# A decoder trunk on one core: the weight tiles and four sums move by 1728 bytes in SBUF, to the offset of h

## The chip, the cores and the metric

The kernel runs on one core of a Trainium2 chip. The metric is the device time of one execution in microseconds (us). Before the change it is 2354.61 us, the median of three runs (2351.29, 2354.61, 2356.11).

## The reference

Two layers of a decoder over 256 tokens of width 2048, all in float32. Layer 0 mixes tokens with a causal Conformer convolution, layer 1 with gated linear attention (GLA); each mixer is followed by a SwiGLU feed-forward net (FFN) of width 5632. Norms stand before and after each, and a vector `c` gives shifts, scales and gates.

```python
def swiglu_ffn(h, w_in, w_out):
    gate, up = jnp.split(h @ w_in, 2, axis=-1)
    return (jax.nn.silu(gate) * up) @ w_out

def reference(x, c, w_ada, b_ada, ...):
    c_act = jax.nn.silu(c)
    for i in range(DEPTH):
        mod = c_act @ w_ada[i] + b_ada[i]
        sh1, sc1, gt1, sh2, sc2, gt2 = jnp.split(mod[:, None, :], N_MOD, axis=-1)
        h = rms_norm(x, pre_mix_g[i]) * (1.0 + sc1) + sh1
...
            y = conformer_conv(h, ...)   # i even
...
            y = gla_mixer(h, ...)        # i odd
        x = x + gt1 * rms_norm(y, post_mix_g[i])
        h = rms_norm(x, pre_ffn_g[i]) * (1.0 + sc2) + sh2
        y = swiglu_ffn(h, ffn_w_in[i], ffn_w_out[i])
        x = x + gt2 * rms_norm(y, post_ffn_g[i])
    return x
```

## The kernel before

**Layout.** Activations lie transposed: 128 features to the partitions, 16 blocks `k` of features, 256 tokens along a row. The modulated input of each product, `h`, is kept as two float32r parts, a high one and the low rest, side by side: `h[:, k, 0, :]` and `h[:, k, 1, :]`, 2048 bytes a block and partition, 32768 in all. The FFN's inner result `m` and the GLA's gated output `oo` have the same form.

**Weights.** All weights come in tiles of 1 MB, `raw`, 128 partitions of 8192 bytes, in an order made up front by `tile_order`. Six buffers of the pool `rawp` hold them; every seventh tile of the first 130 goes to a buffer of its own in another pool (`cv`), far behind. `cast_upto` cuts a tile into two halves of eight 128x128 blocks, and splits each half: ScalarE writes the high part `hi` (L398), VectorE the rest `lo` (L399). The pools `hip` and `lop` have three buffers of 4096 bytes each. Tiles of `w_ada` take another way: VectorE multiplies them by `cb` and sums the rows (L364).

**Products.** `product` (L423 to L486) multiplies block by block. For a block of weights it issues two matmuls (L484): `hi` as the stationary operand against high and low part of the activations, 512 columns wide, and `lo` against the high part alone, 256 wide. This document calls them a wide and a narrow matmul, and both together a pair. The order of the two turns with each `k`, so that the two wide matmuls of neighbouring blocks stand next to each other, and the two narrow ones. The blocks of a half are 512 bytes apart in `hi` and `lo`; in the stage `r` the block of `k` is number `k` modulo 8 of its half. The first eight output blocks of four products (`pw2`, `in00`, `aqk`, `in10`) are packed: three matmuls of 256 columns each for a block (L439 to L441), 384 in a stage. In the first product, `pw1`, and in `v` the roles change: `h` is the stationary operand and `hi` or `lo` moves, 512 columns wide (L855 to L862, L1088 to L1090).

**Stages.** `pw1`, convolution, `pw2`; FFN of layer 0 (`in00`, `out00`, `in01`, `out01`); GLA (`aqk`, gates, `v` with the scores `s`, `r` with the attention `po`, `wo`); FFN of layer 1. Between them stand junctions, which renew `x` and make the next `h`. A matmul of float32 operands, such as `po`, stands twice in the trace, one record for each of its two passes.

**Where tiles lie.** The pool `const` is laid out in the order of its tiles, and the pools `rawp`, `hip`, `lop` and `tmp` follow. Bytes from a partition's start, in the program before: `h` 61024; then `masks` (1024 bytes), `inv_d`, `two_d`, `inv_e`, `mhalf` (32 each, with what they are rounded up by), `der` (512) and `ab` (64), 1728 together; then the sums `s_y`, `s_z`, `s_xz`, `s_xx` (1024 each) from 95520; the six `raw` buffers from 99616, three `hi` from 148768, three `lo` from 161056. The separate `raw` buffer is at 212640, `m` at 183904, `oo` at 190048, `cb` at 52064. Modulo 2048, `h`, `m` and `oo` start at 1632, and `raw`, `hi` and `lo` at 1312.

Of the kernel before, what the change touches and what calls it, by code (L numbers as in the profile page):

```python
# [7 lines left out]
F32 = mybir.dt.float32  # L8
F32R = mybir.dt.float32r
I8 = mybir.dt.int8  # L10
# [4 lines left out]
P = 128  # L15
D = 2048
KD = D // P
# [130 lines left out]
def trunk(ctx: ExitStack, tc: tile.TileContext, a: dict, out: bass.AP):  # L148
    nc = tc.nc

    const = ctx.enter_context(tc.tile_pool(name="const", bufs=1))
    rawp = ctx.enter_context(tc.tile_pool(name="rawp", bufs=6))
    hip = ctx.enter_context(tc.tile_pool(name="hip", bufs=3))
    lop = ctx.enter_context(tc.tile_pool(name="lop", bufs=3))
    tmp = ctx.enter_context(tc.tile_pool(name="tmp", bufs=2))
    ps = ctx.enter_context(tc.tile_pool(name="ps", bufs=4, space=PSUM))
    ps2 = ctx.enter_context(tc.tile_pool(name="ps2", bufs=1, space=PSUM))
# [27 lines left out]
    mod = const.tile([P, 2 * 6 * KD], F32, tag="mod", name="mod")  # L185
    h = const.tile([P, KD, 2, T], F32R, tag="h", name="h")
    h_hi, h_lo = h[:, :, 0, :], h[:, :, 1, :]
    masks = const.tile([P, 8, P], I8, tag="masks", name="masks")
    for j in range(4):
        s = slice(j * 512, (j + 1) * 512)  # L190
        pc = ps.tile([P, 512], F32, tag="mm", name=f"cb{j}")
# [10 lines left out]
    def cols(name, i, n):  # L202
        return par[:, COLS[name][0] + i : COLS[name][0] + i + n]

    inv_d = const.tile([P, 1], F32, tag="inv_d", name="inv_d")
    nc.vector.memset(inv_d, 1.0 / D)
    two_d = const.tile([P, 1], F32, tag="two_d", name="two_d")
    nc.vector.memset(two_d, 2.0 / D)
    inv_e = const.tile([P, 1], F32, tag="inv_e", name="inv_e")
    nc.vector.memset(inv_e, HEADS / D)  # L210
    mhalf = const.tile([P, 2], F32, tag="mhalf", name="mhalf")
    nc.vector.memset(mhalf, -0.5)
    der = const.tile([P, 8, KD], F32, tag="der", name="der")
    ab = const.tile([P, KD], F32, tag="ab", name="ab")

    s_y = const.tile([P, T], F32, tag="s_y", name="s_y")
    s_z = const.tile([P, T], F32, tag="s_z", name="s_z")
# [1034 lines left out]
```

## Time and profile before

| | before |
|---|---|
| runs, us | 2351.29, 2354.61, 2356.11 |
| profiled execution, us | 2356.34 |
| its span, us | 2354.6 |
| mean granted TensorE clock | 0.993 |
| DMA moved | 605.50 MB, mean 257 GB/s |

The span reaches from the first to the last instruction on the core; the profiled execution's own time is 1.7 us longer. PE is TensorE's matmul side and PEld its weight loads; DVE is VectorE, ACT ScalarE, POOL GpSimd. The duration of a matmul in the profile includes its way through the array, so neighbours overlap: what a matmul costs in a stream is the distance from its start to the next one's start, or a stretch of time divided by the matmuls that stand in it. In the rows of the timeline neighbours of one kind are put together: "x2" are two instructions, the first time is the start of the first.

### The profile page before, as it was taken

The numbers are of one execution on the slowest core, as the hardware profiler recorded it, in microseconds if no ns is written. First come the engines' busy times: TensorE is split into PE (matmuls) and PEld (weight loads), VectorE is DVE, ScalarE is ACT, GpSimd is POOL, SyncE is SP. The second block draws the span as 40 slices with busy tenths as digits, with TensorE's granted clock in tenths as the row PEclk, the third lists the DMA queues.
The fourth block names the chain that finished last, engine by engine and source line by source line (L and its number), as shares of the span: only waits on it lengthen the run. The fifth ranks groups of instructions, "written<-read, shape, count | busy, mean of one in ns | idle before, by whom it ended". The sixth has DMA issues, their size and how long they took to land.

```text
span 2354.6 us, 34894 instructions
## 1 busy us (share of the span) xinstructions
PE 2310.3 (98%) x14028; PEld 1999.0 (85%) x14028; DVE 1770.8 (75%) x2520; ACT 1113.3 (47%) x1677; POOL 26.4 (1%) x27
## 2 busy tenths in 40 slices
PE   8999999999999999999999999999999999999997
PEld 5777679998888888888898888889888888888886
DVE  5777859888877788889988878898666555666665
ACT  5333236654444444444456545554544444444442
POOL 0000000000000000000000000000000000000001
PEclk9999999999999999999999999999999999999998
DMA  9988967378878787888844556774565665665651
GB/s 379 418 334 336 377 270 291 139 268 310 312 295 320 300 316 295 318 302 308 300 162 161 215 217 228 259 260 148 212 228 204 230 228 204 230 228 203 231 192 59
DMA packets 85100, 605.50 MB, mean 257 GB/s; under 512 B 9573, under 2 KB 9957, under 8 KB 12101
## 3 DMA queue, kind: packets, MB, share of 16 engines
q1 hardware_dynamic: 84938, 603.28, 68.8%
q8 instruction: 110, 1.80, 0.3%
q14 instruction: 52, 0.43, 0.0%
HBM read 601.14 MB, written 2.10 MB: 256 GB/s over the span
## 4 chain that ended last, share of the span: by engine, by line
PE 94%; DVE 3%; ACT 1%; DMA 1%; issue 1%; POOL 0%; POOLq 0%; SPq 0%; DVEq 0%; ACTq 0%
PE in L484 38%; PE out L484 20%; PE r L484 4%; PE wo L484 4%; PE pw L484 2%; PE aqk L484 1%; PE v L1088 1%; PE v L1089 1%; PE v L1090 1%; PE s L1037 1%; PE in_pair L440 1%; PE in_pair L441 1%; PE in_pair L439 1%; DVE lo L399 1%; PE pw L861 1%; PE pw L862 1%
## 5 line engine op out<-in xcount | busy, mean ns | idle before, releaser
L398 ACT CAST hi<-raw 128x1024 fp32r<-128x1024 f32 x754 | 790.3, 1051 | 995.7 <-PE in L484 279.6
L399 DVE TENSOR_TENSOR lo<-raw,hi 128x1024 fp32r<-128x1024 f32 x754 | 919.6, 1222 | 453.6 <-ACT hi L398 452.6
L484 PE MATMUL in<-h,hi 128*128 128x512 f32 x2560 | 795.1, 392 | 0.2 <-DVE gate L938 0.2
L484 PEld LDWEIGHTS in<-h,lo 128*128 128x128 f32 x2560 | 480.7, 188 | 105.7
L484 PE MATMUL in<-h,lo 128*128 128x256 f32 x2560 | 505.2, 279 | 0.0
L484 PE MATMUL out<-m,hi 128*128 128x512 f32 (+1 forms) x1452 | 438.8, 385 | 0.0
L484 PEld LDWEIGHTS in<-h,hi 128*128 128x128 f32 x2560 | 388.0, 188 | 0.4 <-DVE gate L938 0.4
L364 DVE SCALAR_TENSOR_TENSOR raw<-raw,cb 128x2048 f32<-128x2048 f32 x159 | 362.8, 2284 | 0.0
L484 PEld LDWEIGHTS out<-m,lo 128*128 128x128 f32 x1408 | 263.5, 188 | 55.3 <-DVE lo L399 0.9
L484 PE MATMUL out<-m,lo 128*128 128x256 f32 x1408 | 281.0, 279 | 0.1
L484 PEld LDWEIGHTS out<-m,hi 128*128 128x128 f32 x1452 | 224.0, 188 | 2.1
L484 PE MATMUL wo<-oo,hi 128*128 128x512 f32 (+1 forms) x272 | 80.5, 379 | 1.4 <-ACT hi L398 1.4
L484 PE MATMUL r<-h,hi 128*128 128x512 f32 x256 | 81.6, 396 | 0.0
L498 DVE TENSOR_TENSOR join<-in,join 128x256 f32<-128x256 f32 x160 | 66.6, 416 | 0.0
L440 PE MATMUL in_pair<-h,hi 128*128 128x256 f32 x240 | 64.3, 279 | 0.7 <-DVE h L555 0.7
L441 PE MATMUL in_pair<-h,lo 128*128 128x256 f32 x240 | 62.6, 278 | 0.0
L439 PE MATMUL in_pair<-h,hi 128*128 128x256 f32 x240 | 59.3, 278 | 1.9 <-ACT h L554 1.9
L497 ACT COPY join<-in 128x256 f32<-128x256 f32 x160 | 58.4, 365 | 0.0
L484 PEld LDWEIGHTS wo<-oo,lo 128*128 128x128 f32 x256 | 47.9, 188 | 9.6
L484 PEld LDWEIGHTS r<-h,lo 128*128 128x128 f32 x256 | 47.7, 188 | 9.9
L484 PE MATMUL wo<-oo,lo 128*128 128x256 f32 x256 | 51.9, 279 | 0.0
L484 PE MATMUL r<-h,lo 128*128 128x256 f32 x256 | 51.7, 282 | 0.0
(424 smaller groups left out, 2841.9 us busy)
## 6 DMA issues: line engine op xcount, KB each, us to landing
raw<-in_in_dram SPq DMA_DIRECT2D x176, 1024.0 KB, 5.0
raw<-in_w_ada_dram SPq DMA_DIRECT2D x159, 1024.0 KB, 5.5
raw<-in_out_dram SPq DMA_DIRECT2D x88, 1024.0 KB, 5.1
raw<-in_pw_dram SPq DMA_DIRECT2D x48, 1024.0 KB, 8.3
raw<-in_aqk_dram SPq DMA_DIRECT2D x17, 1024.0 KB, 4.8
raw<-in_w_ada_s_dram SPq DMA_DIRECT2D x16, 1024.0 KB, 11.7
raw<-in_w_ada_r_dram SPq DMA_DIRECT2D x16, 1024.0 KB, 7.9
raw<-in_v_dram SPq DMA_DIRECT2D x16, 1024.0 KB, 4.8
```

Of the source, the lines that this page charges most:

```text
L364: nc.vector.scalar_tensor_tensor(out=raw, in0=raw, scalar=1.0, in1=cb, op0=ALU.mult, op1=ALU.mult, accum_out=modcol(name, i))
L398: nc.scalar.copy(hi, part)
L399: done = nc.vector.tensor_tensor(out=lo, in0=part, in1=hi.bitcast(F32), op=ALU.subtract)
L439: nc.tensor.matmul(acc, w_hi, x_hi, start=False, stop=False, skip_group_check=True)
L440: nc.tensor.matmul(acc, w_hi, x_lo, start=False, stop=False, skip_group_check=True)
L441: nc.tensor.matmul(acc, w_lo, x_hi, start=False, stop=closes, skip_group_check=True)
L484: nc.tensor.matmul(dst, weight, moving, start=n == 0 and i == 0, stop=end and i == len(parts) - 1, skip_group_check=ob not in narrow,)
L497: nc.scalar.copy(dst, acc[:, T:])
L498: nc.vector.tensor_tensor(out=dst, in0=acc[:, :T], in1=dst, op=ALU.add)
L861: nc.tensor.matmul(acc, h_hi[:, k, n], w_lo[:, s], start=False, stop=False, skip_group_check=shared)
L862: nc.tensor.matmul(acc, h_lo[:, k, n], w_hi[:, s], start=False, stop=k == KD - 1, skip_group_check=shared)
L1037: nc.tensor.matmul(sps[:, c], lhs[:, j, c], rhs[:, j, c], start=j == 0, stop=j == 1)
```

## The change

A new pool, `small`, stands behind `lop` and ahead of `tmp`. `masks`, `inv_d`, `two_d`, `inv_e`, `mhalf`, `der` and `ab` are taken from it in place of `const`.

```diff
     lop = ctx.enter_context(tc.tile_pool(name="lop", bufs=3))
+    small = ctx.enter_context(tc.tile_pool(name="small", bufs=1))
     tmp = ctx.enter_context(tc.tile_pool(name="tmp", bufs=2))
...
-    masks = const.tile([P, 8, P], I8, tag="masks", name="masks")
+    masks = small.tile([P, 8, P], I8, tag="masks", name="masks")
...
-    inv_d = const.tile([P, 1], F32, tag="inv_d", name="inv_d")
+    inv_d = small.tile([P, 1], F32, tag="inv_d", name="inv_d")
...
-    two_d = const.tile([P, 1], F32, tag="two_d", name="two_d")
+    two_d = small.tile([P, 1], F32, tag="two_d", name="two_d")
...
-    inv_e = const.tile([P, 1], F32, tag="inv_e", name="inv_e")
+    inv_e = small.tile([P, 1], F32, tag="inv_e", name="inv_e")
...
-    mhalf = const.tile([P, 2], F32, tag="mhalf", name="mhalf")
+    mhalf = small.tile([P, 2], F32, tag="mhalf", name="mhalf")
...
-    der = const.tile([P, 8, KD], F32, tag="der", name="der")
-    ab = const.tile([P, KD], F32, tag="ab", name="ab")
+    der = small.tile([P, 8, KD], F32, tag="der", name="der")
+    ab = small.tile([P, KD], F32, tag="ab", name="ab")
```

Every instruction stays: on each engine the same instructions stand in the same order with the same waits, and each has the same shapes. What differs is addresses. In bytes from a partition's start:

| tile | before | after | before, modulo 2048 | after, modulo 2048 |
|---|---|---|---|---|
| h | 61024 | 61024 | 1632 | 1632 |
| s_y | 95520 | 93792 | 1312 | 1632 |
| raw, first of six | 99616 | 97888 | 1312 | 1632 |
| hi, first of three | 148768 | 147040 | 1312 | 1632 |
| lo, first of three | 161056 | 159328 | 1312 | 1632 |
| masks | 93792 | 171616 | 1632 | 1632 |
| der | 94944 | 172768 | 736 | 736 |
| temporaries (`tmp`) | 173344 | 173344 | 1312 | 1312 |
| m | 183904 | 183904 | 1632 | 1632 |
| oo | 190048 | 190048 | 1632 | 1632 |
| separate raw | 212640 | 212640 | 1696 | 1696 |

1728 is 27 times 64 and three times 512 and 192 more. So the offset modulo 64 is the same for every tile (32 for those that move), and modulo 512 the weight blocks go from 192 bytes past those of `h` to the same offset.

## The prediction

> **What bounds the kernel.** The page first: the busy shares, and the chain of waits that ended last by engine.
>
> ```profile
> span 2354.6 us, 34894 instructions
> PE 2310.3 (98%) x14028; PEld 1999.0 (85%) x14028; DVE 1770.8 (75%) x2520; ACT 1113.3 (47%) x1677; POOL 26.4 (1%) x27
> PE 94%; DVE 3%; ACT 1%; DMA 1%; issue 1%; POOL 0%; POOLq 0%; SPq 0%; DVEq 0%; ACTq 0%
> ```
>
> TensorE matmuls are 98% of the span and 94% of the chain. So the time is the number of matmuls times the pace at which they follow each other. The number is not touched. The question is whether addresses set the pace, and the next view answers part of it: stretches of time with the matmuls that stand in each (the x behind PE's busy time; then PEld, DVE, ACT, POOL, clock, DMA share, GB/s).
>
> ```profile
> 50.00:340.00 290.00, 276.35 (x1703) 202.76 (x1702) 210.05 (x308) 95.63 (x139) 0.69 (x1) 0.98 0.88 351
> 808.00:1050.00 242.00, 242.00 (x1405) 212.93 (x1404) 195.66 (x229) 117.68 (x175) 0.00 (x0) 1.00 0.82 308
> 1973.00:2215.00 242.00, 242.00 (x1405) 213.08 (x1404) 153.31 (x189) 117.34 (x175) 0.00 (x0) 1.00 0.62 220
> ```
>
> The second and third row are the same stage of the two FFNs (`in01`, `in11`). PE never rests, and both have 1405 matmuls in 242 us: 172.2 ns a matmul, 344.5 ns a pair of wide and narrow. VectorE is busy 195.66 us in one and 153.31 in the other, the DMA engines 0.82 and 0.62 of the time. So other engines' traffic in SBUF doesn't reach TensorE's pace; if addresses do, it is by what TensorE reads itself: the moving operand, and the weights that it loads meanwhile.
>
> How many pairs this is about, by the groups of L484 (wide matmuls; some rows hold a few narrow ones):
>
> ```profile
> L484 PE MATMUL in<-h,hi 128*128 128x512 f32 x2560 | 795.1, 392 | 0.2 <-DVE gate L938 0.2
> L484 PE MATMUL out<-m,hi 128*128 128x512 f32 (+1 forms) x1452 | 438.8, 385 | 0.0
> L484 PE MATMUL wo<-oo,hi 128*128 128x512 f32 (+1 forms) x272 | 80.5, 379 | 1.4 <-ACT hi L398 1.4
> L484 PE MATMUL r<-h,hi 128*128 128x512 f32 x256 | 81.6, 396 | 0.0
> ```
>
> Together 4540. One ns a pair is 4.5 us, 0.2% of the time, which is about what a measurement of this kernel can tell from no change.
>
> **Is the pace a matter of offsets?** Here is TensorE's timeline in `r`. Each row is two neighbours; the pace is the distance between starts.
>
> ```profile
> 1432.15 0.39 PE L484 MATMUL r<-h,lo 128*128 128x256 f32 x2
> 1432.37 0.62 PE L484 MATMUL r<-h,hi 128*128 128x512 f32 x2
> 1432.83 0.40 PE L484 MATMUL r<-h,lo 128*128 128x256 f32 x2
> 1433.07 0.62 PE L484 MATMUL r<-h,hi 128*128 128x512 f32 x2
> 1433.53 0.28 PE L484 MATMUL r<-h,lo 128*128 128x256 f32 x1
> 1433.64 0.50 PE L507 MATMUL sso<-inv_e,s_z 128*128 128x1 f32 x4
> ...
> 1434.67 0.39 PE L484 MATMUL r<-h,lo 128*128 128x256 f32 x2
> 1434.89 0.62 PE L484 MATMUL r<-h,hi 128*128 128x512 f32 x2
> 1435.35 0.40 PE L484 MATMUL r<-h,lo 128*128 128x256 f32 x2
> 1435.59 0.62 PE L484 MATMUL r<-h,hi 128*128 128x512 f32 x2
> 1436.05 0.39 PE L484 MATMUL r<-h,lo 128*128 128x256 f32 x2
> ...
> 1436.73 0.40 PE L484 MATMUL r<-h,lo 128*128 128x256 f32 x2
> ```
>
> The first narrow pair is of blocks 0 and 1 (k), the next of 2 and 3; the single one at 1433.53 is block 4. They take 0.22 us (1432.15 to .37) and 0.24 (.83 to 1433.07). That looks like an effect of the weights' place: blocks 0 and 4 of a half lie 2048 bytes apart, and the pattern repeats every four blocks. But then four short matmuls of another kind (`sso`) are put between. Behind them blocks 6 and 7 take 0.22 (1434.67 to .89), and 8 and 9 take 0.24 (1435.35 to .59): the same offsets, modulo 2048, have swapped their times. And the four blocks from 1435.35 to 1436.73 take 1.38 us, 345 ns a pair, as in the FFN's windows. So the unevenness hangs on the place in the instruction stream, not on the address, and it only shifts time between neighbours.
>
> The packed stages say the same more plainly. They run one code over the same offsets of `h` and of the weights; here are three of the four:
>
> ```profile
> 352.00:382.00 30.00, 30.00 (x257) 30.00 (x256) 28.96 (x38) 17.31 (x27) 0.00 (x0) 1.00 0.82 304
> 450.00:480.00 30.00, 30.00 (x267) 30.00 (x267) 29.13 (x48) 17.33 (x26) 0.00 (x0) 1.00 0.57 206
> 1196.00:1226.00 30.00, 30.00 (x257) 30.00 (x256) 26.83 (x41) 16.25 (x22) 0.00 (x0) 1.00 0.50 176
> ```
>
> `pw2` and `aqk` run 257 matmuls in 30 us (116.7 ns each), `in00` 267 (112.4). Equal offsets, paces 3.7% apart: the pace has two modes, and something other than the offset chooses.
>
> What these rows cannot show is a product of float32r operands at the new relation. Before, each weight block stands 192 bytes past a block of `h`, modulo 512, in every row above; after, at 0. The nearest case is `z`, eight matmuls whose two operands (`at`, `wgu`) both lie at 1632 modulo 2048:
>
> ```profile
> 1244.09 0.41 PE L996 MATMUL z<-at,wgu 96*128 96x256 f32 x2
> 1244.33 0.28 PE L484 MATMUL aqk<-h,lo 128*128 128x256 f32 x1
> ...
> 1249.90 0.41 PE L996 MATMUL z<-at,wgu 96*128 96x256 f32 x2
> 1250.15 0.28 PE L484 MATMUL aqk<-h,lo 128*128 128x256 f32 x1
> ```
>
> Two of them take 0.24 and 0.25 us, 120 and 125 ns each, against 110 to 120 for the narrow ones above. But they use 96 rows of the array and are thrown in between others, which disturbs the pattern as `sso` did. I read them as no sign, and keep their price for a rival.
>
> **The change, part by part.**
> - *Stationary operand in the L484 products, 192 bytes to 0 from the moving one.* Between 0 (the two modes and the swap above) and the rivals' prices below. I take 0.
> - *Moving operand in `pw1` and `v`,* now at the offset that `h` has as moving operand elsewhere. The row pair
>
> ```profile
> 1320.71 0.39 PE L1090 MATMUL v<-hi,h 128*128 128x512 f32 x1
> 1324.91 0.39 PE L1090 MATMUL v<-hi,h 128*128 128x512 f32 x1
> ```
>
> has 18 matmuls in 4.20 us, 233 ns each; in `r` a wide one takes 230 (1432.37 to .83 is two). If the offset made the 3 ns, `v` (384 matmuls by the code) and `pw1` (some 600) would gain 3 us. I take 0, since the order of loads differs as well, and keep 3 us for the range.
> - *Which mode a packed stage falls into.* By the two paces 4.3 ns times 384 matmuls is 1.7 us a stage. Three stages could turn fast (`pw2`, `aqk` and `in10`, which I count with the slow ones: 5 us less) or `in00` slow (1.7 more). I take 0.
> - *Splits and sums on ScalarE and VectorE (L398, L399, L364).* `raw`, `hi` and `lo` move together; to `cb` the distance changes. The trace has that experiment already, since every seventh `raw` lies elsewhere:
>
> ```profile
> 376.03 2.28 DVE L364 SCALAR_TENSOR_TENSOR raw<-raw,cb 128x2048 f32<-128x2048 f32 x1
> 381.64 2.29 DVE L364 SCALAR_TENSOR_TENSOR raw<-raw,cb 128x2048 f32<-128x2048 f32 x1
> 387.29 2.28 DVE L364 SCALAR_TENSOR_TENSOR raw<-raw,cb 128x2048 f32<-128x2048 f32 x1
> ```
>
> The middle one is tile 119 of the order, 17 times seven, in the separate buffer (160 modulo 512, not 288): 2.29 us beside 2.28. So 0; a hundredth would lie under TensorE's work, with VectorE at 75%. Should that cover go, 159 such instructions at 0.01 are 1.6 us.
> - *DMA writes into `raw`.* The offset modulo 64 stays. Only the first stage could feel them: there PE has 290.00 less 276.35, 13.65 us, of idle time with the DMA engines at 0.88. One per cent of that stage is 2.9 us, either way. I take 0.
> - *`masks`, `der`, `ab` and the small constants:* the same instructions read them from another place, some tens of times; 0.
>
> Sum: the profiled execution took 2356.3 us (span 2354.6 and 1.7 around it) and stays there; it lies 1.7 above the median of the runs. So I forecast the median as it was, **2354.6 us**.
>
> **A rule that gives another room.** In `r`, po's two-pass matmuls follow the rows above:
>
> ```profile
> 1438.11 0.59 PE L1108 MATMUL po<-sc,y 128*128 128x256 f32 x2
> 1438.54 0.38 PE L1109 MATMUL po<-sc,y 128*128 128x128 f32 x2
> ```
>
> 0.215 us each, if a float32 pass over 256 columns streams as long as a wide float32r matmul, against 0.230 of that one. The Trainium skill's page "TensorE: Matmul & The Clock Gate", section "Back-to-back issue gap", gives 216 ns for 512 columns and 109 for 256, warm: 325 a pair, an estimate by that page; the trace has 344.5. By it the sum would be 19.5 ns times 4540 lower, 89 us, if offsets cost the difference. The same page, in "Step-by-step: what each phase is for", says that loading weights takes no read bandwidth from the running matmul, which leaves offsets nothing to cost; no row here shows which holds.
>
> **Rivals.**
> - *Faster: part of the pace above is a collision of weight load and moving read, and it goes.* For: the pair takes 0.230 and 0.115 where `po` suggests 0.215 for the wide one. Against: the swap in `r`, and the two modes at equal offsets. With the nearest row, all narrow matmuls at the 0.22 for two of the quick ones: 5 ns less on average, 4540 times, 23 us: 2332. All the way to po's pace (15 and 7.5 ns a pair) it would be 102 us: 2252.
> - *Slower: equal offsets collide.* Mechanism: while a narrow matmul streams, the next weights must be loaded, with almost no slack; if both read the same piece of SBUF at once, the load ends later and the next matmul with it. Place: every narrow and packed matmul. For: z's 120 and 125 ns. Against: they are only eight, out of their pattern. Price: 122.5 less 115, 7.5 ns a narrow matmul, 34 us: 2389. It decides from 1 ns on. Confined to the 1536 packed ones (122.5 less 116.7) it is 9 us: 2363.
>
> **Numbers.** No difference 0.76 (2354.6); faster 0.13 (2332); slower 0.11 (2389). Faster by over 0.2%: 0.13; within 0.2%: 0.76; slower: 0.11. The range: down by 3 us of run spread (2351.3), 5 of packed modes and 3 of `v` and `pw1` to 2343; up to 2363, the slower rival confined to packed stages, which also covers run spread (2356.1), 1.7 and the 2.9 of DMA. Beyond lie most of both rivals, some 0.2.
>
> **What would show it.** After the change the windows of `in01` and `in11` should again have 1405 matmuls in 242 us within 3, four blocks in `r` 1.38 us, the packed stages 257 or 267 in 30 us, L364 2.28. Wrong it is if the FFN's windows hold over 1410 or under 1400; then offsets do set TensorE's pace. If they agree and the time doesn't, the first stage's DMA is to be looked at.

## The result: 0.6% slower, and TensorE's pace is where it went

The changed kernel takes 2371.55 us (median of 4 runs, 2368.39 to 2374.19), the kernel before 2355.36 us (4 runs beside them, 2351.29 to 2357.26). The ratio is 1.0063, with a 95% interval from 1.0049 to 1.0078. The profiled execution took 2374.19 us, its span 2372.4 us: 17.8 us more than before.

The page of the changed kernel shows span, busy time, the chain by engine, and the groups that answer to those shown of before. Line numbers are one higher.

```profile
span 2372.4 us, 34894 instructions
PE 2330.3 (98%) x14028; PEld 2010.8 (85%) x14028; DVE 1772.7 (75%) x2520; ACT 1111.6 (47%) x1677; POOL 25.3 (1%) x27
PE 95%; DVE 2%; ACT 1%; DMA 1%; issue 1%; POOL 0%; POOLq 0%; SPq 0%; ACTq 0%; DVEq 0%
...
L485 PE MATMUL in<-h,hi 128*128 128x512 f32 x2560 | 804.7, 395 | 0.1
L365 DVE SCALAR_TENSOR_TENSOR raw<-raw,cb 128x2048 f32<-128x2048 f32 x159 | 363.1, 2286 | 0.5 <-DMA raw<-in_w_ada_dram 0.5
L485 PE MATMUL out<-m,hi 128*128 128x512 f32 (+1 forms) x1452 | 443.7, 388 | 0.0
L485 PE MATMUL wo<-oo,hi 128*128 128x512 f32 (+1 forms) x272 | 81.6, 383 | 1.4 <-ACT hi L399 1.4
L485 PE MATMUL r<-h,hi 128*128 128x512 f32 x256 | 82.4, 398 | 0.0
```

PE's busy time grew by 20.0 us (2310.3 to 2330.3), more than the span; VectorE and ScalarE stayed within 2 us. Every group of wide matmuls is longer, by 2 to 4 ns each, with the same counts. The same stretches of time as before, in the columns told there:

```profile
50.00:340.00 290.00, 277.09 (x1715) 205.10 (x1714) 211.99 (x310) 96.98 (x144) 0.69 (x1) 0.98 0.88 353
808.00:1050.00 242.00, 242.00 (x1390) 211.14 (x1390) 193.12 (x227) 115.32 (x171) 0.00 (x0) 1.00 0.82 307
1973.00:2215.00 242.00, 242.00 (x1392) 211.19 (x1391) 150.57 (x183) 114.96 (x169) 0.00 (x0) 1.00 0.61 219
...
352.00:382.00 30.00, 30.00 (x252) 30.00 (x252) 27.66 (x32) 16.56 (x24) 0.00 (x0) 1.00 0.86 318
450.00:480.00 30.00, 30.00 (x252) 30.00 (x251) 28.00 (x46) 15.63 (x23) 0.00 (x0) 1.00 0.52 190
1200.00:1230.00 30.00, 30.00 (x252) 30.00 (x252) 28.59 (x46) 16.63 (x23) 0.00 (x0) 1.00 0.54 186
```

Look at the x behind PE. `in01` and `in11` hold 1390 and 1392 matmuls in 242 us where they held 1405: 348 ns a pair, 3.5 more. PE is busy the whole time and the clock is granted in full, so it is the pace and nothing that PE waits for. Three packed stages are shown; each runs 252 in 30 us (119 ns each), and the fourth, `in10`, goes at the same pace from start to start. The two modes of before, 257 and 267, are gone. Only the first stage got further (x1715, was 1703); e2 below has 1717 there with TensorE's operands in their old place, so that is not their doing.

The timeline of `in01` shows what a row of two neighbours takes, first before, then after:

```profile
900.20 0.40 PE L484 MATMUL in<-h,lo 128*128 128x256 f32 x2
900.44 0.62 PE L484 MATMUL in<-h,hi 128*128 128x512 f32 x2
900.90 0.39 PE L484 MATMUL in<-h,lo 128*128 128x256 f32 x2
901.13 0.62 PE L484 MATMUL in<-h,hi 128*128 128x512 f32 x2
901.58 0.40 PE L484 MATMUL in<-h,lo 128*128 128x256 f32 x2
```

```profile
859.85 0.40 PE L485 MATMUL in<-h,lo 128*128 128x256 f32 x2
860.09 0.63 PE L485 MATMUL in<-h,hi 128*128 128x512 f32 x2
860.55 0.39 PE L485 MATMUL in<-h,lo 128*128 128x256 f32 x2
860.78 0.63 PE L485 MATMUL in<-h,hi 128*128 128x512 f32 x2
861.25 0.40 PE L485 MATMUL in<-h,lo 128*128 128x256 f32 x2
```

Four blocks take 1.40 us (859.85 to 861.25), not 1.38 (900.20 to 901.58). The rows of narrow ones take 0.24 and 0.23 as before; the rows of wide ones now 0.46 and 0.47, where they took 0.46 and 0.45. And `v`, where the roles change:

```profile
1328.55 0.39 PE L1091 MATMUL v<-hi,h 128*128 128x512 f32 x1
1332.64 0.39 PE L1091 MATMUL v<-hi,h 128*128 128x512 f32 x1
```

18 matmuls in 4.09 us, 227 ns each, where they took 233. So one move made most products slower and `v` faster.

By stage, from the start of a stage's first matmul to that of the next (worked out from the starts in both traces):

| stage | before, us | after, us | difference |
|---|---|---|---|
| up to `pw1` | 31.4 | 31.1 | -0.3 |
| `pw1`, convolution | 310.2 | 308.2 | -2.0 |
| `pw2` and junction | 98.9 | 101.7 | +2.8 |
| FFN of layer 0, junction | 743.4 | 750.7 | +7.3 |
| `aqk` | 103.9 | 104.4 | +0.5 |
| `v` | 117.1 | 115.1 | -2.0 |
| `r` | 101.4 | 102.1 | +0.7 |
| `wo` and junction | 99.0 | 102.5 | +3.5 |
| FFN of layer 1 to the end | 749.3 | 756.6 | +7.3 |

The sum is the 17.8 us of the span. Each row is one trace against one, and `pw1` and the junctions scatter: e2 below, where TensorE's operands stand as before, also has 2.4 us less in `pw1` and 2.7 more in `pw2` with its junction. Adding the distances from start to start by kind of matmul, over the whole trace, is safer. The products of L485 take 15.9 us more, 3.3 ns a pair; the packed matmuls 3.4: their pace, 120.0 ns from 117.8 and in `in00` from 113.4, costs 4.7, and waits among them shrank by 1.3. (The windows give 1 ns less, since matmuls that reach over a window's ends are counted in full.) `v` gives back 2.0. That is 17.3 us. In `pw1` the matmuls of 512 columns became quicker, as in `v` (median 234 to 230 ns), and those of 256 slower (114 to 120), which leaves 0.5 us less.

### The profile page after: what moved, and what is told of

It reads as the page before. It is cut to its first block, busy times and chain, and to the rows that moved or that the text cites. A ratio compares the mean times of both kernels' runs of the same rounds, so it can differ in the third digit from the quotient of the medians.

```text
span 2372.4 us, 34894 instructions
## 1 busy us (share of the span) xinstructions
PE 2330.3 (98%) x14028; PEld 2010.8 (85%) x14028; DVE 1772.7 (75%) x2520; ACT 1111.6 (47%) x1677; POOL 25.3 (1%) x27
## 4 chain that ended last, share of the span: by engine, by line
PE 95%; DVE 2%; ACT 1%; DMA 1%; issue 1%; POOL 0%; POOLq 0%; SPq 0%; ACTq 0%; DVEq 0%
PE in L485 38%; PE out L485 21%; PE r L485 4%; PE wo L485 4%; PE pw L485 2%; PE aqk L485 1%; PE v L1089 1%; PE v L1090 1%; PE v L1091 1%; PE s L1038 1%; PE in_pair L441 1%; PE in_pair L442 1%; PE in_pair L440 1%; PE pw L862 1%; PE pw L856 1%; PE pw L863 1%
## 5 line engine op out<-in xcount | busy, mean ns | idle before, releaser
L399 ACT CAST hi<-raw 128x1024 fp32r<-128x1024 f32 x754 | 789.9, 1050 | 1017.2 <-issue 296.7
L485 PE MATMUL in<-h,hi 128*128 128x512 f32 x2560 | 804.7, 395 | 0.1
L485 PEld LDWEIGHTS in<-h,lo 128*128 128x128 f32 x2560 | 480.9, 188 | 113.6
L485 PE MATMUL in<-h,lo 128*128 128x256 f32 x2560 | 502.9, 278 | 0.0
L485 PE MATMUL out<-m,hi 128*128 128x512 f32 (+1 forms) x1452 | 443.7, 388 | 0.0
L485 PEld LDWEIGHTS in<-h,hi 128*128 128x128 f32 x2560 | 390.0, 189 | 0.3 <-DVE gate L939 0.3
L365 DVE SCALAR_TENSOR_TENSOR raw<-raw,cb 128x2048 f32<-128x2048 f32 x159 | 363.1, 2286 | 0.5 <-DMA raw<-in_w_ada_dram 0.5
L485 PEld LDWEIGHTS out<-m,lo 128*128 128x128 f32 x1408 | 263.8, 188 | 58.4 <-DVE lo L400 0.8
L485 PE MATMUL out<-m,lo 128*128 128x256 f32 x1408 | 281.1, 279 | 0.0
L485 PEld LDWEIGHTS out<-m,hi 128*128 128x128 f32 x1452 | 225.8, 189 | 2.4
L485 PE MATMUL wo<-oo,hi 128*128 128x512 f32 (+1 forms) x272 | 81.6, 383 | 1.4 <-ACT hi L399 1.4
L485 PE MATMUL r<-h,hi 128*128 128x512 f32 x256 | 82.4, 398 | 0.0
L485 PEld LDWEIGHTS wo<-oo,lo 128*128 128x128 f32 x256 | 48.0, 188 | 10.3
L485 PEld LDWEIGHTS r<-h,lo 128*128 128x128 f32 x256 | 47.7, 188 | 10.4
L485 PE MATMUL wo<-oo,lo 128*128 128x256 f32 x256 | 51.8, 279 | 0.0
L485 PE MATMUL r<-h,lo 128*128 128x256 f32 x256 | 51.5, 281 | 0.0
```

Of the source, the lines that this page charges most:

```text
L365: nc.vector.scalar_tensor_tensor(out=raw, in0=raw, scalar=1.0, in1=cb, op0=ALU.mult, op1=ALU.mult, accum_out=modcol(name, i))
L399: nc.scalar.copy(hi, part)
L485: nc.tensor.matmul(dst, weight, moving, start=n == 0 and i == 0, stop=end and i == len(parts) - 1, skip_group_check=ob not in narrow,)
```

## The experiments

In all runs the instructions of every engine and their order stay as they are; only addresses change. They all compute the whole of the reference. Diffs are against the changed kernel unless said otherwise. The windows row shown is that of `in01`, 808 to 1050 us.

**e1: the same distance modulo 512, another modulo 2048.**

```diff
-    masks = small.tile([P, 8, P], I8, tag="masks", name="masks")
+    masks = const.tile([P, 8, P], I8, tag="masks", name="masks")
-    der = small.tile([P, 8, KD], F32, tag="der", name="der")
+    der = const.tile([P, 8, KD], F32, tag="der", name="der")
```

> Here masks and der go back to const; weights lie 1536 bytes behind their place after the change: still at the offset of h modulo 512 (0 apart), but 1536 apart modulo 2048. Theory R (the pace depends on the distance of stationary and moving operand modulo 512): as after the change, 1390 matmuls in 242 us of in01, wide 233 ns, v 227 to 230, ratio 1.006. Theory M (the distance counts modulo 2048 or more): something else, up to before's 1405, wide 229, v 233, ratio 1.000.

Ratio 1.0055 (1.0040 to 1.0070).

```profile
808.00:1050.00 242.00, 242.00 (x1392) 211.14 (x1390) 193.08 (x227) 115.26 (x172) 0.00 (x0) 1.00 0.82 308
```

1392 matmuls, as after the change, and the distances from start to start are the same too (table below). So what the address does, it does modulo 512 or a part of it. Theory M falls.

**e2: only `raw` and the sums at the new place.**

```diff
     rawp = ctx.enter_context(tc.tile_pool(name="rawp", bufs=6))
+    small = ctx.enter_context(tc.tile_pool(name="small", bufs=1))
     hip = ctx.enter_context(tc.tile_pool(name="hip", bufs=3))
     lop = ctx.enter_context(tc.tile_pool(name="lop", bufs=3))
-    small = ctx.enter_context(tc.tile_pool(name="small", bufs=1))
```

> Here only raw and the four sums stand where they are after the change; hi and lo stand where they were before. Theory R and theory A (the absolute offset of a TensorE operand counts): as before, 1405 matmuls in 242 us of in01, v 233, ratio 1.000. Theory O (the splits, sums or DMA writes at new addresses cost it): as after, ratio 1.006.

Ratio 1.0000 (0.9991 to 1.0010).

```profile
808.00:1050.00 242.00, 242.00 (x1405) 213.08 (x1404) 195.05 (x229) 117.51 (x175) 0.00 (x0) 1.00 0.81 307
```

As before. `raw`, the DMA writes into it, ScalarE's and VectorE's reads of it and the four sums cost nothing at the new place. Theory O falls; `hi` and `lo` are left, which TensorE reads.

**e3: h moves to the weights in place of the weights to h.** Against the kernel before, `h` is taken from `const` behind `ab`, and so lies 1728 bytes further on; the weights, `m` and `oo` stay.

```diff
-    h = const.tile([P, KD, 2, T], F32R, tag="h", name="h")
-    h_hi, h_lo = h[:, :, 0, :], h[:, :, 1, :]
...
     ab = const.tile([P, KD], F32, tag="ab", name="ab")
+    h = const.tile([P, KD, 2, T], F32R, tag="h", name="h")
+    h_hi, h_lo = h[:, :, 0, :], h[:, :, 1, :]
```

> Here h moves to the offset of the weights (288 modulo 512), and weights, m and oo stay as before. Theory R: products from h as after the change (in01 1390 matmuls in 242 us, wide 233; v 227 to 230), products from m and oo as before (out wide 229); in all about +10 us, ratio 1.004. Theory A (the absolute offset modulo 512 counts: weights at 96 slow, at 288 fast, moving at 96 fast): v as before, 233, in01 as before or, since the moving h now lies at 288, slower than 1405; out as before.

Ratio 1.0035 (1.0024 to 1.0046). The groups of this run, shapes kept apart (behind the first bar: busy us, mean ns of one), and its window:

```profile
L484 PE MATMUL in<-h,hi 128*128 128x512 f32 x2560 | 804.7, 395 | 0.1
L484 PE MATMUL out<-m,hi 128*128 128x512 f32 x1364 | 423.6, 392 | 0.0
L1090 PE MATMUL v<-hi,h 128*128 128x512 f32 x128 | 50.5, 394 | 0.0
...
808.00:1050.00 242.00, 242.00 (x1392) 211.22 (x1391) 193.62 (x227) 116.07 (x173) 0.00 (x0) 1.00 0.81 303
```

The groups of before that answer to the second and third of these:

```profile
L484 PE MATMUL out<-m,hi 128*128 128x512 f32 x1364 | 423.5, 392 | 0.0
L1090 PE MATMUL v<-hi,h 128*128 128x512 f32 x128 | 50.9, 398 | 0.0
```

This is the run that decides. Here the weights have not moved at all, and yet `in` is as slow as after the change (804.7 us, 1392 matmuls) and `v` as quick (394, with 398 before). `out`, whose moving operand `m` stayed, is as before. Theory A leaves room for a slow `in`, since `h` has moved, but not for a quick `v`; the distance of the two operands explains both. Theory R holds, theory A falls.

**e4: hi at h's offset, lo 192 bytes from it.**

```diff
     hip = ctx.enter_context(tc.tile_pool(name="hip", bufs=3))
+    small = ctx.enter_context(tc.tile_pool(name="small", bufs=1))
     lop = ctx.enter_context(tc.tile_pool(name="lop", bufs=3))
-    small = ctx.enter_context(tc.tile_pool(name="small", bufs=1))
```

> Here raw, sums and hi stand as after the change (hi 0 from h modulo 512), lo as before (192 from it). Theory R, own operand: every wide matmul 233 as after (its weights are hi), narrow as before, about +17 us. Theory R, load: a wide matmul is slow when the weights loaded meanwhile are 0 apart; lo is loaded in every second one, so half of them 229 and half 233, about +8 us.

Ratio 1.0045 (1.0031 to 1.0060).

```profile
808.00:1050.00 242.00, 242.00 (x1398) 212.44 (x1397) 194.10 (x228) 116.29 (x173) 0.00 (x0) 1.00 0.81 305
```

In `in01` a wide matmul behind which `hi` is loaded takes 231.5 ns, and one behind which `lo` is loaded 228.8 (table). Both have `hi` as their own weights, at distance 0, and after the change they took 232.9 and 233.4. So a matmul's own weights are not what makes it slow; the distance of the weights loaded meanwhile from what it reads fits, as the second theory has it. (In this trace's `in01` the load of the next weights starts 3 ns after the matmul does, by the median, and is recorded with 188 ns.) The pair takes 346.7 ns there, half-way between before and after, and the same in `in00` and `in11`. In `in10` it takes 353.4, though: the same distances, another mode, which neither theory had. Its 576 pairs at 6.7 ns more are 3.9 us, and bring the second theory's 8 us near the measured 0.45%, which is 11 us.

**e5 to e8: other distances.** `ab` alone stays in `const` (64 bytes); the four one-column tiles (128); `tmp` goes ahead of `rawp` (10560 bytes, 320 modulo 512); `tmp` ahead and `ab` in `const` (384). As an example, e7:

```diff
+    tmp = ctx.enter_context(tc.tile_pool(name="tmp", bufs=2))
     rawp = ctx.enter_context(tc.tile_pool(name="rawp", bufs=6))
     hip = ctx.enter_context(tc.tile_pool(name="hip", bufs=3))
     lop = ctx.enter_context(tc.tile_pool(name="lop", bufs=3))
     small = ctx.enter_context(tc.tile_pool(name="small", bufs=1))
-    tmp = ctx.enter_context(tc.tile_pool(name="tmp", bufs=2))
```

> The weights lie 64 bytes past the offset of h modulo 512 (only ab stays in const). Theory S (each distance modulo 512 has its own pace, as a weight load meets the moving read at other times): neither as before nor as after; in01 outside 1403 to 1407 matmuls in 242 us and off 1390. Theory Z (only equal offsets collide, all others are alike): as before, 1405, v 233 to 235 ns, ratio 1.000.

> 128 bytes past the offset of h modulo 512. Theory S: another pace than at 0, 64 and 192; if it runs smoothly from 0 (1390) to 192 (1405), about 1400 in 242 us. Theory Z: 1405, v 233 to 235, ratio 1.000.

> 320 bytes past the offset of h modulo 512 (tmp goes ahead of rawp). For the products with weights as stationary operand this distance is one that no run had; seen from v, where the roles change, it is 192, which the other products had before. Theory S with the distance alone: v gets a pace of its own, apart from 235 (at 320) and 230 (at 0); in01 off 1405. Theory Z: 1405 and v 235, ratio 1.000.

> 384 bytes past the offset of h modulo 512. Theory S: another pace of its own, between 1385 and 1425 matmuls in 242 us of in01. Theory Z: 1405, v 235, ratio 1.000.

Ratios 1.0018 (1.0008 to 1.0029), 1.0089 (1.0074 to 1.0104), 1.0019 (1.0010 to 1.0028) and 1.0068 (1.0052 to 1.0085). The row of each, in this order:

```profile
808.00:1050.00 242.00, 242.00 (x1397) 212.27 (x1396) 193.49 (x228) 116.47 (x173) 0.00 (x0) 1.00 0.82 309
...
808.00:1050.00 242.00, 242.00 (x1391) 211.81 (x1390) 193.09 (x226) 115.73 (x171) 0.00 (x0) 1.00 0.82 307
...
808.00:1050.00 242.00, 242.00 (x1398) 212.31 (x1398) 194.05 (x227) 116.46 (x174) 0.00 (x0) 1.00 0.82 305
...
808.00:1050.00 242.00, 242.00 (x1391) 211.80 (x1390) 193.94 (x224) 115.43 (x170) 0.00 (x0) 1.00 0.81 305
```

Theory Z falls, as none has 1405. The pace goes with the distance, but not smoothly: 64 has 1397 matmuls, and 128 falls back to 1391, with the pair of distance 0 (348.3 ns) made up of other parts. Nor has every distance a pace of its own, as theory S has it: the first and third row, and the second and fourth, agree, down to a tenth of a ns in the table: 64 and 320, 128 and 384. They differ by 256. (The ratios of 128 and 384 differ by 0.2%; their intervals overlap.)

**e9: 256 bytes from h, 192 from m and oo.** The four one-column tiles and `ab` stay in `const`, and `ab` takes twice its room.

```diff
-    ab = small.tile([P, KD], F32, tag="ab", name="ab")
+    ab = const.tile([P, 2 * KD], F32, tag="ab", name="ab")[:, :KD]
```

> The weights lie 256 bytes past the offset of h modulo 512, and m and oo move by 64, so that the weights are 192 from these. Theory P (the distance counts modulo 256, since 64 and 320 ran alike, and 128 and 384): products from h as after the change (in01 1390 to 1392 matmuls in 242 us, v 230), products from m and oo as before (out wide 229, not 233); about +10 us, as with h alone moved. Theory Q (modulo 512): in01 has a pace of its own, off 1390 to 1392.

Ratio 1.0042 (1.0027 to 1.0057).

```profile
L485 PE MATMUL in<-h,hi 128*128 128x512 f32 x2560 | 804.7, 395 | 0.1
L485 PE MATMUL out<-m,hi 128*128 128x512 f32 x1364 | 423.5, 392 | 0.0
...
808.00:1050.00 242.00, 242.00 (x1392) 211.19 (x1391) 192.72 (x227) 115.44 (x171) 0.00 (x0) 1.00 0.83 308
```

`in` as after the change, `out` as before, in one kernel, as theory P forecast. The distance counts modulo 256.

**e10, e11: 160 and 224, steps of 32 bytes.** In e10 `inv_d`, `two_d`, `inv_e` and `ab` stay in `const`; in e11 `tmp` goes ahead as well.

> The weights lie 160 bytes past the offset of h modulo 512, between 128 (1391 matmuls in 242 us of in01) and 192 (1405). Theory F (every step of 32 bytes has its own pace): off both values, if it runs smoothly about 1398. Theory G (only pieces of 64 bytes count): like 128 or like 192, 1391 or 1405 within 2. A start of raw at a multiple of 256 has no price of its own by either.

> The weights lie 480 bytes past the offset of h modulo 512, 224 modulo 256, between 192 (1405 matmuls in 242 us of in01) and 0 (1390). Theory F: off both, about 1398 if smooth. Theory G: 1405 or 1390 within 2, and the other one than 160 bytes gives if that falls to 128's side.

Ratios 1.0158 (1.0143 to 1.0173) and 1.0050 (1.0032 to 1.0068).

```profile
808.00:1050.00 242.00, 242.00 (x1372) 210.50 (x1371) 191.06 (x223) 113.87 (x169) 0.00 (x0) 1.00 0.82 302
...
808.00:1050.00 242.00, 242.00 (x1398) 213.40 (x1397) 194.05 (x227) 116.35 (x172) 0.00 (x0) 1.00 0.83 309
```

Steps of 32 bytes matter too (theory F), and 160 is the worst of all: 1372 matmuls, 37 us over the kernel before, 32 bytes from the distance of before. The smooth 1398 was missed there and met at 224.

**e12: a distance for each, chosen from the runs.** `hi` 64, `lo` 192 bytes from `h`: `ab` stays in `const`, and the four one-column tiles come from a pool `few` between `hip` and `lop`.

```diff
     hip = ctx.enter_context(tc.tile_pool(name="hip", bufs=3))
+    few = ctx.enter_context(tc.tile_pool(name="few", bufs=1))
     lop = ctx.enter_context(tc.tile_pool(name="lop", bufs=3))
```

> hi lies 64 bytes past the offset of h, lo 192. Theory add (what a matmul takes hangs on the distance of the weights loaded meanwhile alone, so times of the runs at 64 and 192 add up): wide with hi loaded 226, wide with lo 230.5, narrow with hi 113.3, narrow with lo 116.7, 343.3 a pair, 1410 matmuls in 242 us, about 7 us faster than before. Theory mix (a load's end also hangs on the loads ahead of it): no such sum, 1397 to 1405, as before or slower.

Ratio 1.0007 (0.9998 to 1.0017): no difference that can be told.

```profile
808.00:1050.00 242.00, 242.00 (x1398) 214.51 (x1397) 194.59 (x228) 116.70 (x174) 0.00 (x0) 1.00 0.82 306
```

The wide ones got what was hoped for, 225.8 and 229.2 ns. The narrow ones took it back, 118.3 and 120.0 against 113.3 and 116.7. Loads do not add up one by one, as theory mix has it. And the even ratio is a balance: added up from start to start as above, the products of L486 take 6.8 us more than before, while the packed matmuls take 4.3 less (113.5 to 113.7 ns in all four stages) and `v` 1.0 less.

Mean distances from a matmul's start to the next one's, ns, worked out from the starts in each trace (over 260 counted as 260). "hi" and "lo" are the weights of the next matmul, x the matmuls in 242 us; the distance is that of the weights from `h`, modulo 256:

```
run            distance   in01: x  wide hi,lo   narrow hi,lo  pair   in10   out   v
                                                                     pair   wide  wide
before         192        1405  227.5 230.3  115.5 116.7  345.0  345.1  229.2 235.1
e2 (raw)       192        1405  227.3 230.7  115.5 116.5  345.0  345.0  229.2 235.1
after          0          1390  232.9 233.4  115.8 114.6  348.3  348.4  232.9 230.2
e1 (1536)      0          1392  232.9 233.3  115.8 114.6  348.3  348.3  232.9 230.2
e3 (h moved)   0          1392  232.6 233.5  115.9 114.6  348.3  348.4  229.3 230.9
e9 (256)       0          1392  232.9 233.3  115.8 114.6  348.3  348.4  229.2 230.9
e5 (64)        64         1397  225.9 235.8  113.3 118.3  346.7  346.7  231.1 231.9
e7 (320)       64         1398  225.8 235.9  113.3 118.3  346.7  346.7  231.1 231.9
e6 (128)       128        1391  227.5 234.6  118.3 116.2  348.3  348.4  231.6 234.6
e8 (384)       128        1391  227.5 234.6  118.3 116.3  348.3  348.4  231.6 234.7
e10 (160)      160        1372  236.7 230.8  120.8 118.3  353.3  350.0  233.4 235.9
e11 (480)      224        1398  226.6 229.2  120.0 117.5  346.7  346.7  230.7 235.0
e4             0, lo 192  1398  231.5 228.8  115.6 117.4  346.7  353.4  230.6 231.6
e12            64, lo 192 1398  225.8 229.2  118.3 120.0  346.7  346.7  228.3 232.6
```

None of these layouts beats the kernel before.

## Why the prediction was wrong

- **What bounds the kernel** was right. The pace of TensorE sets the time, and the windows of `in01` and `in11` told it: they fell under 1400, which the prediction had named as the sign that offsets set the pace.
- **The step that failed** is the one from the swap in `r` to "hangs on the place in the instruction stream, not on the address", and from there to the 0 for "stationary operand in the L484 products". What it saw is true: equal addresses can take either time, and four blocks take 1.38 us all the same. But the weight blocks that it compared lie multiples of 512 bytes from one another, and so do the blocks of `h`, while what counts is the distance from weights to `h` modulo 256. In the whole trace of before, the relation that the change alters stood at one value in those products. Rows that all share a value can't show what it does. The prediction said that the new relation wasn't in its rows, and then took the 0 all the same, with 0.76.
- **The two modes of the packed stages** were taken to mean that something else than the offset sets the pace. After the change all four stages run at one pace, 120 ns from start to start. The offset decides which modes there are. What chooses between them at 192 stayed open; it is neither the addresses of these operands nor the stage alone, since in e2, with both as before, `in00` runs at 117.8 ns and `in10` at 113.3, the other way round than before (113.4 and 117.8).
- **z** was read as no sign. Its 120 and 125 ns, at distance 0, were not far from the 120 that the packed stages show at distance 0; whether for the same reason, no run shows.
- **The slower rival** had the right kind of cause, a weight load against the moving read, and e4 points to the load's part. For the packed matmuls it had the sign right: they take 2.2 to 6.6 ns more, 3.4 us in all, where it had 9. For the pairs its place and its rule were wrong. It put the price on the narrow matmuls, 7.5 ns; in `in01` the narrow ones got 0.9 ns quicker (116.1 to 115.2, means of the table's columns), the wide ones 4.2 slower (228.9 to 233.1). And equal offsets are not the worst: 160 is slower, and for `v` 0 is the best of all. That the load waits for the read, rather than the read for the load, is not shown.
- **`pw1` and `v`:** of the 3 us kept for the range, `v` gave 2.0. `pw1` gave 0.5, as its matmuls of 256 columns became slower; the 2.0 us that its stage lost came in e2 too. The prediction took 0 for both.
- **Splits, sums, DMA, constants at 0:** right. e2 has the ratio 1.0000 with `raw` and the sums moved; L365 takes 2286 ns, with 2284 before.
- **The rule of the Trainium skill** (page "TensorE: Matmul & The Clock Gate", section "Step-by-step: what each phase is for") that loading weights takes no read bandwidth from the running matmul was read as leaving offsets nothing to cost. For these float32r matmuls they cost something: between distances of 160 and 192 bytes a pair of `in01` differs by 8.3 ns. Whether it is read bandwidth that is lost, no run shows. The 325 ns a pair, an estimate from the section "Back-to-back issue gap" of the same page of the Trainium skill, whose formula is for a matmul on its own, was reached by no layout; the best is 345.

## What to carry to other kernels

Where TensorE is busy all the time and loads weights for every matmul, the distance between the weights and the moving operand in a partition, modulo 256 bytes, is a knob worth a few runs: here, with float32r operands, it was worth from 0 to 1.6% with nothing else touched. The best distance was not the same for every kind of matmul: 192 for the pairs, `hi` at 64 for the packed ones (113.4 to 113.7 ns, in three stages of four with `lo` at 64 too, in all four with `lo` at 192), 0 for `v`; a layout that gives each its own was not tried. Any edit that adds or moves a small tile ahead of such operands turns that knob unasked, so look at the operands' addresses before a small loss or gain is put down to the edit itself. And before a trace is used to rule out a cause, ask whether that cause varies anywhere in it.

## What was not expected of the hardware

- The pace depends on the distance of the operands modulo 256 bytes: 64 and 320 bytes give 225.8, 235.9, 113.3 and 118.3 ns alike within 0.1; 0 and 256, and 128 and 384, also agree.
- Steps of 32 bytes count: in `in01` 353.3 ns a pair at 160 bytes, 345.0 at 192, 346.7 at 224.
- The pair's mean in the `in` stages takes few values, 345.0, 346.7, 348.3, 350.0 and 353.3, all a multiple of 1.67 ns apart, and one distance can have two of them: 346.7 and 353.4 in e4, 353.3 and 350.0 in e10, stage against stage. What chooses stays open.
- At the granted clock of 1.00, other engines' load does not show in it: `in01` and `in11` had 1405 matmuls both with the DMA engines at 0.82 and at 0.62. How SBUF is built that this comes out, and why `v` and the packed matmuls have other best distances than the pairs, stays open.
